# Leaving TensorE's order to the scheduler instead of the program text, in a hybrid attention encoder step

## The chip, the cores and the metric

The kernel runs on one core of a Trainium2 chip, as one launch. The metric is device time in microseconds (us) from the first to the last instruction of the program with what lies around it; a run's time is that of its slowest core, here the only one.

## What is computed

One step of a one-layer streaming encoder in float32, for 1024 prompt frames and 64 sample frames (which also see 512 cached frames), width 1024:

```python
h = x + 0.5 * rmsnorm(swiglu(rmsnorm(x, g_pre_ff1), w_gate1, w_up1, w_down1), g_post_ff1)
u = rmsnorm(h, g_pre_mix) @ w_in                 # 256 + 128 + 32 + 3*512 columns
# group A, 8 heads: latent attention, softmax over chunk-causal scores
s = (q_lat @ latent.T + q_rope @ krope.T) * MLA_SCALE
o_mla = softmax(where(visible, s, -inf)) @ latent @ w_uv
# group B, 8 heads: stick-breaking attention, strictly causal
z = (q @ k.T) * SB_SCALE
tail = reverse_cumsum(log_sigmoid(-z)) - log_sigmoid(-z)
o_sb = where(before, exp(log_sigmoid(z) + tail), 0) @ v
h = h + rmsnorm(concat(rmsnorm(o_mla), rmsnorm(o_sb)) @ w_out, g_post_mix)
h = h + 0.5 * rmsnorm(swiglu(rmsnorm(h, g_pre_ff2), w_gate2, w_up2, w_down2), g_post_ff2)
y = rmsnorm(h, g_final)                          # and the new cache rows
```

The feed-forward width is 2816. Each swiglu is down(silu(gate) * up).

## The kernel before

**Tiling.** The frames are split into two groups: G1 of 576 (512 prompt, 64 sample) in columns of 288, and G2 of 512. Features lie on the 128 partitions, frames along the free dimension. Each float32 product is made of three fp32r matmuls of a high and a low part (`mm3`, `steps`: hi x hi, hi x lo, lo x hi); a weight tile `wr` comes from HBM, ACT casts it to `wh` (L139) and DVE subtracts to get `wl` (L140).

**Two streams of work.** The feed-forward (`ffn`) is a generator that yields after every matmul; its results go to three PSUM banks of their own, tile `f`. The rest is the mixing work: `finish` (residual and norm sums after a feed-forward), `premix`, `project` (u @ w_in and what hangs on it), `attend` (scores in tile `s`, transposes in `t`, weighted values in `v`), `mix_out` (w_out, residual, norm). It uses the other five banks, handed out in turn by `bank_m`. The program's order is: feed-forward 1 of G1; then mixing of G1 with feed-forward 1 of G2 as filler; then mixing of G2 with feed-forward 2 of G1 as filler; then feed-forward 2 of G2. So the stages follow each other along the span: first feed-forward alone, then project, attention and mix_out of G1 with filler, the same of G2 with filler, then feed-forward alone again.

**The reckoned clock.** The text keeps a time of its own, `self.clock`. Every matmul adds its reckoned duration; every mixing step says when its operands will be there and calls `wait`, which writes filler matmuls until the clock has come that far:

```python
            self.clock += max(n / 2400 + 0.013, 0.11)
...
    def wait(self, t):
        while self.clock < t:
            mark = self.clock
            if next(self.filler, BLOCKED) is BLOCKED:
                self.clock = max(t, mark)
...
    def evict(self, n):
        self.busy = max(self.busy, self.clock) + SLACK * (n / 960 + 0.15)
        self.free[self.turn] = self.busy + 0.3
```

`chain` (L639) gives the reckoned time after which a score bank is free again, `took` (L650) the time after which transposes have been read. At the end of a stage the filler can be blocked: `prep2` (L1143), which makes the input of feed-forward 2 of G1, needs the sum `rx` that `mix_out` ends with.

**Who sets the order.** The kernel is written for a layer that records all instructions, finds their dependencies and then gives each engine its order. For DVE, ACT, POOL and SP a scheduler in that layer picks the order: it runs through the recorded program with durations that it assumes, and whenever an engine is free it takes, of the instructions whose operands it holds for ready, the one that was written first. `tc.manual_schedule(engines={PE})` in `build` (L1269) exempts TensorE: its matmuls stand in exactly the order in which the text wrote them. Every engine executes its own order strictly; an instruction whose operand is late holds up all behind it.

Lines that matter below: `mul` L154 and `turn_over` L158 issue all matmuls and transposes; `stick` L593 (L610, L613 and L619 are its DVE steps, the last two the scan); `weighted` L659 (L679 and L680 read the transposes into `ph` and `pl`, which the `v` matmuls take); `rsqrt` L221 (a matmul with `ones` sums the squares over partitions, as in s<-rx,ones); `residual` L272 (the DMA of L275 into tile `e`, the additions of L277).

Of the kernel before, what the change touches and what calls it, by code (L numbers as in the profile page):

```python
# [1261 lines left out]
def build(nc, arrays):  # L1262
    a = {k: nc.dram_tensor("in_" + k, v.shape, mybir.dt.from_np(v.dtype), kind="ExternalInput").ap()
         for k, v in arrays.items()}
    for k, s in OUTS.items():
        a[k] = nc.dram_tensor("out_" + k, list(s), F32, kind="ExternalOutput").ap()
    a["xT"] = [a["xT0"], a["xT1"]]
    with tile.TileContext(nc) as tc:
        with ExitStack() as ctx, tc.manual_schedule(engines={mybir.EngineType.PE}):  # L1269
            body(tc, a, ctx)  # L1270


# [19 lines left out]
```

## Time and profile before

| what | value |
|---|---|
| runs | 2451.69, 2444.57, 2450.37 us; median 2450.37 us |
| profiled execution | 2446.7 us; its span 2444.9 us |
| PE (matmuls) | 2285.4 us busy, 93% of the span, 13869 instructions |
| PEld (weight loads) | 2057.0 us, 84% |
| DVE, ACT, POOL | 1428.3 us (58%), 1291.1 us (53%), 94.7 us (4%) |
| granted TensorE clock, mean | 0.981 |
| DMA | 268.79 MB, mean 110 GB/s |

The span is from the first to the last instruction; the profiled execution's own time has 1.8 us around it. A busy engine counts every stretch in which at least one of its instructions is under way. A wait in the profile is idle time of an engine, put down to the instruction whose end released the next one.

### The profile page before, as it was taken

What the parts mean: (1) busy time and instruction counts of PE and PEld (TensorE: products, weight loads), DVE (VectorE), ACT (ScalarE), POOL (GpSimd) and SP (SyncE); (2) the same over time, 40 slices, a digit from 0 to 9 for tenths busy, and PEclk for the clock granted to TensorE, in tenths of its full rate; (3) what the DMA queues carried; (4) which work ended last, traced back from release to release, by engine and by line L of the source; (5) the groups of instructions that cost most, each with busy time, mean ns of one, the idle gap of its engine ahead of it and who ended that gap; (6) DMA issues with size and microseconds to landing.
All of it is one profiled execution on the core that took longest, in us unless ns stands there. A gap on an engine that the chain in (4) does not pass through costs nothing. (4 is left out here: it accounts for less than half of the span.)

```text
span 2444.9 us, 37638 instructions
## 1 busy us (share of the span) xinstructions
PE 2285.4 (93%) x13869; PEld 2057.0 (84%) x13869; DVE 1428.3 (58%) x2464; ACT 1291.1 (53%) x2498; POOL 94.7 (4%) x270
## 2 busy tenths in 40 slices
PE   8999999989999999997999999989999989999997
PEld 7999999878977777786788998988889788888885
DVE  6444444763167777745674367877776477444445
ACT  6534333552377777644452478777776345433333
POOL 1000000010000000000110000000000010000001
PEclk9999999999999999998999999999999999999998
DMA  6322222624453343233345532323221324333321
GB/s 205 114 88 84 81 80 86 203 95 149 143 160 112 105 120 114 76 135 121 109 143 176 174 91 72 92 76 103 75 70 57 129 88 128 129 98 97 94 92 35
DMA packets 186614, 268.79 MB, mean 110 GB/s; under 512 B 59216, under 2 KB 68048, under 8 KB 186400
## 3 DMA queue, kind: packets, MB, share of 16 engines
q1 hardware_dynamic: 186432, 266.41, 34.5%
q8 instruction: 109, 1.79, 0.3%
q14 instruction: 73, 0.60, 0.1%
HBM read 227.61 MB, written 40.88 MB: 110 GB/s over the span
## 5 line engine op out<-in xcount | busy, mean ns | idle before, releaser
L154 PE MATMUL f<-xh,wh 128*128 128x288 f32 (+1 forms) x2112 | 698.6, 331 | 3.0 <-ACT xh L139 2.8
L154 PE MATMUL f<-xl,wh 128*128 128x288 f32 (+1 forms) x2112 | 698.5, 331 | 1.9 <-POOL xl L140 0.9
L154 PE MATMUL f<-xh,wl 128*128 128x288 f32 (+1 forms) x2112 | 698.8, 331 | 0.0
L139 ACT CAST wh<-wr 128x512 fp32r<-128x512 f32 x638 | 383.8, 618 | 535.3 <-PE f L154 362.5
L140 DVE TENSOR_TENSOR wl<-wr,wh 128x512 fp32r<-128x512 f32 x638 | 435.0, 695 | 265.6 <-ACT wh L139 229.0
L154 PEld LDWEIGHTS f<-xh,wh 128*128 128x128 f32 x2112 | 400.8, 190 | 33.7 <-ACT xh L139 3.3
L154 PEld LDWEIGHTS f<-xl,wh 128*128 128x128 f32 x2112 | 400.5, 190 | 33.0 <-POOL xl L140 2.9
L154 PEld LDWEIGHTS f<-xh,wl 128*128 128x128 f32 x2112 | 401.2, 190 | 28.7 <-issue 1.5
L154 PE MATMUL f<-hh,wh 128*128 128x288 f32 (+2 forms) x1072 | 351.8, 328 | 3.4 <-ACT hh L139 2.0
L154 PE MATMUL f<-hl,wh 128*128 128x288 f32 (+2 forms) x1072 | 349.9, 326 | 1.4 <-DVE hl L140 1.4
L154 PE MATMUL f<-hh,wl 128*128 128x288 f32 (+2 forms) x1072 | 350.5, 327 | 0.0
L154 PEld LDWEIGHTS f<-hh,wh 128*128 128x128 f32 x1072 | 202.3, 189 | 19.4 <-ACT hh L139 2.6
L154 PEld LDWEIGHTS f<-hl,wh 128*128 128x128 f32 x1072 | 202.3, 189 | 15.9 <-DVE hl L140 2.4
L154 PEld LDWEIGHTS f<-hh,wl 128*128 128x128 f32 x1072 | 202.3, 189 | 13.0 <-issue 0.5
L319 DVE TENSOR_TENSOR y<-f,y 128x288 f32<-128x288 f32 (+2 forms) x248 | 127.5, 518 | 119.9 <-PE f L154 119.3
L364 DVE TENSOR_TENSOR act<-f,act 128x288 f32<-128x288 f32 (+1 forms) x132 | 70.0, 530 | 126.3 <-ACT act L363 126.2
L680 DVE TENSOR_TENSOR pl<-t,ph 128x384 fp32r<-128x384 f32 (+1 forms) x160 | 98.4, 630 | 36.9 <-ACT ph L679 35.9
L154 PE MATMUL v<-pl,v 128*128 128x256 f32 x320 | 89.4, 302 | 31.9 <-DVE pl L680 31.4
L365 DVE TENSOR_TENSOR act<-f,act 128x288 f32<-128x288 f32 (+1 forms) x132 | 70.2, 532 | 66.5 <-PE f L154 62.3
L154 PE MATMUL s<-kh,qh 128*128 128x256 f32 (+3 forms) x224 | 81.8, 367 | 27.5 <-DVE a L619 17.4
L679 ACT CAST ph<-t 128x384 fp32r<-128x384 f32 (+1 forms) x160 | 83.6, 541 | 41.3 <-PE t L158 39.1
L139 ACT CAST hh<-act 128x288 fp32r<-128x288 f32 (+1 forms) x132 | 65.2, 494 | 75.6 <-DVE act L365 75.3
(307 smaller groups left out, 3495.8 us busy)
## 6 DMA issues: line engine op xcount, KB each, us to landing
wr<-in_wg SPq DMA_DIRECT2D x176, 256.0 KB, 3.0
wr<-in_wu SPq DMA_DIRECT2D x176, 256.0 KB, 3.1
wr<-in_wd SPq DMA_DIRECT2D x176, 256.0 KB, 2.9
wr<-in_win SPq DMA_DIRECT2D x44, 256.0 KB, 3.2
kl<-ks SPq DMA_DIRECT2D x64, 128.0 KB, 2.8
wr<-in_wout SPq DMA_DIRECT2D x32, 256.0 KB, 2.9
h<-y SPq DMA_DIRECT2D x16, 288.0 KB, 2.2
p<-in_xT SPq DMA_DIRECT2D x16, 256.0 KB, 3.2
```

The lines of the kernel that those rows point to most:

```text
L139: nc.scalar.copy(hi, x)
L140: eng.tensor_tensor(lo, x, f(hi), op=ALU.subtract)
L154: self.nc.tensor.matmul(out, lhsT=lhsT, rhs=rhs, start=start, stop=stop)
L319: nc.vector.tensor_tensor(yy, ps[:, :C], yy, op=ALU.add)
L364: nc.vector.tensor_tensor(s, pg[:, :C], s, op=ALU.mult)
L365: nc.vector.tensor_tensor(s, pu[:, :C], s, op=ALU.mult)
L679: nc.scalar.copy(ph[:, end:], tr[:, end:])
L680: nc.vector.tensor_tensor(pl[:, end:], tr[:, end:], f(ph[:, end:]), op=ALU.subtract)
```

## The change

One line: TensorE is no longer exempt. The scheduler now also gives TensorE its order, by the same rule as the other engines: of the matmuls that it holds for ready, the one that the text wrote first. The text, its reckoned clock, the pools, the banks and the tasks are the same, so the same 13686 matmuls are recorded in the same order; that order is now a priority.

```diff
     with tile.TileContext(nc) as tc:
-        with ExitStack() as ctx, tc.manual_schedule(engines={mybir.EngineType.PE}):
+        with ExitStack() as ctx:
             body(tc, a, ctx)
```

What it moves: on TensorE no matmul stands more than 65 places behind its old place and none over 96 ahead of it, but for 35 filler matmuls that now stand 163 to 384 places earlier, at the start of the two mix_outs. In all, 332 runs of one or more matmuls stand earlier than the text has them. The first feed-forward (places 100 to 3098) and the last (12300 to 13500) keep their order. The orders of DVE and ACT change too (by up to 41 places), since the scheduler makes them together with TensorE's; SP's by up to 27.

Three places follow, with the tile numbers of the two programs (those of the change are lower by 2 for the same tile). The first is TensorE at the end of mix_out of G1, where the norm sum of `rx` is taken; before:

```order
L154 MATMUL f_12111<-xh_100,wh_12103 128x512
L154 MATMUL f_12111<-xl_101,wh_12103 128x512
L154 MATMUL f_12111<-xh_100,wl_12102 128x512
L154 MATMUL s_12159<-rx_4982,ones_69 128x288 x2
L154 MATMUL f_12111<-xh_100,wh_12103 128x512
L154 MATMUL f_12111<-xl_101,wh_12103 128x512
```

and now:

```order
L154 MATMUL f_12285<-hh_11205,wh_12268 128x512
L154 MATMUL f_12285<-hl_11206,wh_12268 128x512
L154 MATMUL s_12157<-rx_4980,ones_67 128x288
L154 MATMUL f_12285<-hh_11205,wl_12267 128x512
L154 MATMUL f_12285<-hh_11372,wh_12274 128x512
L154 MATMUL f_12285<-hl_11373,wh_12274 128x512
L154 MATMUL s_12157<-rx_4980,ones_67 128x288
```

The two sums stood in the middle of the gate product f_12111; 62 feed-forward matmuls that stood behind them (the rest of that product, and down products up to the one in tile f_12285) now stand ahead of the first.

The second is TensorE in the attention of G1, at a score group (`s`) of the last head; before:

```order
L154 MATMUL f_10970<-hh_10099,wh_10848 128x512
L154 MATMUL f_10970<-hl_10100,wh_10848 128x512
L154 MATMUL s_10990<-kh_10647,qh_10653 128x384
L154 MATMUL s_10990<-kl_10646,qh_10653 128x384
L154 MATMUL f_10970<-hh_10099,wl_10847 128x512
```

and now:

```order
L154 MATMUL f_11086<-hh_9165,wh_11031 128x512
L154 MATMUL f_11086<-hl_9166,wh_11031 128x512
L154 MATMUL s_10988<-kh_10645,qh_10651 128x384
L154 MATMUL s_10988<-kl_10644,qh_10651 128x384
L154 MATMUL f_11086<-hh_9165,wl_11030 128x512
```

The group stands 30 places later in the whole order, three down products further on in the filler.

The third is DVE in the attention of G2, where `pl` is made for the weighted values (L613 is the scan); before:

```order
L610 SCALAR_TENSOR_TENSOR a_16828<-z_16829,a_16828 128x640
L140 TENSOR_TENSOR hl_16667<-act_16861,hh_16666 128x288
L613 SCALAR_TENSOR_TENSOR a_16828<-z_16829,a_16828 128x639
L680 TENSOR_TENSOR pl_16909<-t_16907,ph_16908 128x512
L680 TENSOR_TENSOR pl_16918<-t_16916,ph_16917 128x512
```

and now:

```order
L140 TENSOR_TENSOR hl_16665<-act_16859,hh_16664 128x288
L680 TENSOR_TENSOR pl_16907<-t_16905,ph_16906 128x512
L610 SCALAR_TENSOR_TENSOR a_16826<-z_16827,a_16826 128x640
L680 TENSOR_TENSOR pl_16916<-t_16914,ph_16915 128x512
L613 SCALAR_TENSOR_TENSOR a_16826<-z_16827,a_16826 128x639
```

The first `pl` stood behind both steps of the scan; it now stands ahead of both, and the second ahead of the scan itself. The `v` matmuls that take them keep their place on TensorE here.

## Rows read from the trace of the kernel before

**Rows 1.** The profile page, part 1: busy time, share of the span, instructions.
```profile
PE 2285.4 (93%) x13869; PEld 2057.0 (84%) x13869; DVE 1428.3 (58%) x2464; ACT 1291.1 (53%) x2498; POOL 94.7 (4%) x270
```

**Rows 2.** Busy time by stretch: length, then engines' us and counts, granted clock, DMA.
```profile
0.00:470.00 470.00, 460.61 (x3305) 449.62 (x3306) 235.35 (x431) 206.58 (x418) 14.45 (x17) 0.99 0.35 112
470.00:690.00 220.00, 202.40 (x1267) 183.31 (x1267) 87.65 (x137) 87.26 (x167) 10.49 (x11) 0.99 0.44 145
690.00:1025.00 335.00, 308.79 (x1625) 250.06 (x1625) 252.22 (x530) 243.53 (x566) 17.18 (x117) 1.00 0.38 112
1025.00:1110.00 85.00, 79.95 (x510) 73.27 (x509) 36.48 (x60) 35.31 (x67) 0.10 (x1) 0.98 0.35 116
1110.00:1200.00 90.00, 72.42 (x306) 58.18 (x305) 53.70 (x76) 36.29 (x63) 6.52 (x4) 0.91 0.36 114
1200.00:1395.00 195.00, 182.24 (x1059) 161.43 (x1058) 105.39 (x169) 84.97 (x165) 13.01 (x8) 0.98 0.50 160
1395.00:1865.00 470.00, 434.49 (x3107) 416.74 (x3106) 353.81 (x577) 354.53 (x633) 14.01 (x93) 0.98 0.27 83
1865.00:1975.00 110.00, 105.94 (x619) 95.01 (x618) 60.73 (x99) 55.60 (x101) 2.83 (x5) 0.96 0.33 110
1975.00:2100.00 125.00, 111.21 (x621) 98.66 (x620) 88.76 (x142) 58.47 (x102) 9.38 (x7) 0.95 0.38 123
2100.00:2445.00 345.00, 327.36 (x1467) 270.74 (x1465) 154.22 (x248) 128.55 (x223) 6.79 (x8) 0.97 0.27 84
```

**Rows 3.** PE's waits over the span, by releaser: us in total, times, longest us.
```profile
PE v L154 <- DVE pl L680: 31.4, 28, 3.3
PE s L154 <- DVE rx L218: 23.3, 2, 15.5
PE s L154 <- DVE a L619: 17.4, 22, 1.2
...
PE s L154 <- ACT a L635: 9.2, 13, 1.5
...
PE t L154 <- DVE tmp L218: 4.5, 1, 4.5
PE t L154 <- issue: 4.1, 1, 4.1
```

**Rows 4.** Timeline, end of mix_out of G1: start us, us, engine, instruction, [idle before].
```profile
1140.82 1.40 POOL L277 TENSOR_TENSOR y<-y,e 128x576 f32<-128x576 f32 x1 [16.25 <-DMA e<-h]
...
1152.72 1.33 PE L154 MATMUL s<-rx,ones 128*128 128x288 f32 x2 [15.51 <-DVE rx L218]
...
1157.04 0.63 PE L154 MATMUL f<-xh,wh 128*128 128x512 f32 x1
1157.47 0.63 PE L154 MATMUL f<-xl,wh 128*128 128x512 f32 x1
...
1160.70 0.39 PE L154 MATMUL f<-hh,wl 128*128 128x512 f32 x1
1160.92 0.39 PE L154 MATMUL f<-hh,wh 128*128 128x512 f32 x1
...
1205.22 0.67 ACT L139 CAST xh<-tmp 128x576 fp32r<-128x576 f32 x1
```

**Rows 5.** Timeline, attention of G1, a score group and what releases it.
```profile
1008.89 0.69 DVE L619 TENSOR_TENSOR_SCAN a<-s,a 128x255 f32<-128x255 f32 x1
...
1009.72 0.41 PE L154 MATMUL s<-kh,qh 128*128 128x384 f32 x1 [0.84 <-DVE a L619]
```

**Rows 6.** Timeline, attention of G2, the place of the third order above.
```profile
1603.38 0.57 ACT L679 CAST ph<-t 128x512 fp32r<-128x512 f32 x1
...
1603.73 0.82 DVE L610 SCALAR_TENSOR_TENSOR a<-z,a 128x640 f32<-128x640 f32 x1
...
1604.83 1.48 DVE L613 TENSOR_TENSOR_SCAN a<-z,a 128x639 f32<-128x639 f32 x1
1606.23 1.26 DVE L680 TENSOR_TENSOR pl<-t,ph 128x512 fp32r<-128x512 f32 x2
...
1606.95 0.39 PE L154 MATMUL v<-pl,v 128*128 128x256 f32 x1 [3.06 <-DVE pl L680]
```

## The prediction

> **What bounds the kernel now.** I read the page's busy times first: PE works 93% of the span, DVE 58%, ACT 53% [rows 1]. So the time is TensorE's work plus TensorE's idle time. The work is the same 13686 matmuls before and after; what the change can alter is the idle time and the clock that the work runs at.
>
> Second, the stretches, because a mean over stages hides where the idle time lies. Length less PE busy gives, in the order of [rows 2]: 9.4, 17.6 (project of G1), 26.2 (attention of G1), 5.1 (mix_out of G1), 17.6 (its end), 12.8 (finish and project of G2), 35.5 (attention of G2), 4.1, 13.8 (mix_out of G2 and its end), 17.6 us (the last feed-forward and the tail): 159.6 us in all. The most that an order could win is about 160 us less what no order can fill, the start and the end.
>
> Third, what the waits are for [rows 3]. In the attention of G2 the `v` matmuls wait for `pl` from DVE, 28 times for 31.4 us. In that of G1 the score matmuls wait for a bank that the scan or the exponential still reads (17.4 and 9.2 us, 35 times). Two norm sums wait for `rx`, 23.3 us. All are alike: the text's clock held an operand for ready, wrote the matmul, and TensorE stood still although filler lay behind it.
>
> **What the change does to each.** It adds and removes no instruction, no DMA and no bank; it only moves. A matmul that the scheduler holds for late is overtaken by filler. So I set each wait against the work put ahead of it. Work is counted at the full clock: a 512-column matmul starts 0.22 us after the one before it [rows 4], the pair at 1160.7; 0.226 over longer runs, a 288-column one after about 0.14 us, 460.6 us by 3305 in the first stretch [rows 2].
>
> *End of mix_out of G1, 17.6 us.* 62 matmuls of 512 columns now stand ahead of the sum: 62 x 0.226 = 14.0 us against a wait of 15.5. But the norm sum before it, t<-acc, stands 15 places later too, so the new cover since then is 47 x 0.226 = 10.6 us, and the residual chain that ends in `rx` waits for its own DMA, e<-h [rows 4], so it does not shorten. Bounds 10.6 and 15.5; I take 11, nearest to the first. What is late next: the input of feed-forward 2, whose last cast ran at 1205 us [rows 4] while its matmuls had begun. That cast waits for the buffer of the other group's input, thus for filler that is itself moved forward, so it moves along.
>
> *Attention of G2, 35.5 us.* Two things help. Before most `v` groups stand 2 to 9 matmuls of 0.14 us now, 0.3 to 1.2 us against waits of some 0.9. Where none do, DVE's order has changed: in [rows 6] `ph` was there at 1603.95, `pl` came only after both steps of the scan (0.82 and 1.48 us), and TensorE stood 3.06 us. Now `pl` is made ahead of them. The scan is delayed in turn; what it feeds is the score chain, which has room here: nearly all score groups of this stage start without a wait (2 of the waits on L635 lie here, 2.6 us). Bounds: 18 us if only the moved matmuls count, each wait against the work ahead of it, 33 if nearly all goes. I take 28, since of the waits without a moved matmul, some 13 us, nearly all are at places where DVE's order has changed in this way.
>
> *Attention of G1, 26.2 us.* Here the gain is smaller than it looks. A score group starts 0.14 us after the scan that frees its bank ends at 1009.58, then 1009.72 [rows 5], and so do most others: the chain score, scan, score sets the pace, and filler put ahead can be counted once, not at each wait. By the last head a score group stands 30 places later: 30 x 0.226 = 6.8 us of filler done early. I take 7; bounds 0 and 17, the sum of each wait against all that stands ahead of it.
>
> *Project of G1, 17.6 us.* Ahead of a waiting product stand 3 to 9 matmuls of the next product or of filler, 0.4 to 1.2 us, against waits mostly of 0.5 to 1; three larger ones keep more than half. I take 8, bounds 0 and 15.
>
> *Finish and project of G2, 12.8 us.* The two norm sums (waits of 4.1 us [rows 3] and 3.0) get 30 and 25 matmuls of 0.14 us ahead, 4.2 and 3.5 us. I take 10, bounds 0 and 12.8.
>
> *Mix_outs and the end of G2's.* G1's mix_out, 5.1 us: 2 (0 to 5). G2's, 4.1 us: 3 (0 to 4). The end of G2's, 13.8 us: 61 matmuls of 288 columns, 8.5 us, ahead of the sum that waited 23.3 - 15.5 = 7.8 us, and 10 ahead of one that waited 4.5: together 11 (0 to 13). Start and tail hardly move: 1 (0 to 2).
>
> Sum: 11 + 28 + 7 + 8 + 10 + 2 + 3 + 11 + 1 = 81 us; ends 29 and 117.
>
> *The clock.* [...] As the waits go, I take 12 back, about half, since some waits stay. Ends 0 and 22.
>
> *New waits.* 332 runs of matmuls, counted in the two orders, stand earlier than before. Where the scheduler holds an operand for ready and it is not, TensorE now waits there. A wait of the usual size is 17.4 / 22 = 0.8 us [rows 3]; one run in 25 gives 13 x 0.8 = 10 us. That is the loss I take, an estimate, ends 0 and 50: the weights and hidden tiles that filler needs are made well ahead in this trace.
>
> Net 81 + 12 - 10 = 83 us. From the profiled execution, 2446.7 us: **2364 us**. That execution lies 3.7 us below the median of the runs, 2450.4, within their spread of 7.
>
> [...] In the attention of G1, TensorE goes through all its banks in turn and stands still 26.2 us in short pieces, yet the granted clock is 1.00 [rows 2]. [...]
>
> **The rivals.**
> 1. *The mixing chain sets the pace in more places.* For it: [rows 5], and the residual chain with its DMA [rows 4]. Then filler put ahead is only counted once per stage and the waits come back further on. The lower ends, 29 us, with 5 of clock: 2447 - 34 = 2413, between 2400 and 2435. Against it: in the attention of G2 the score groups hardly wait. Chance 0.14.
> 2. *Slower: the scheduler is early more often than the text was.* The text's times carry margins; the scheduler's rule has none, and on one in-order queue a filler matmul whose bank or weight is late holds up the score chain behind it. The price is 0.8 us each [rows 3]; it decides from 93 / 0.8 = 116 of the 332 runs, one in three. At 133 it is 106 us, 2447 - 93 + 106 = 2460. Against it: DVE and ACT are at most 75% busy in any stretch [rows 2], and where the trace has a wait the order mostly puts about as much ahead as the wait is long, so the scheduler's times look near the real ones. Chance 0.11.
> 3. *The clock swings.* If the granted clock fell to 0.90 in both attentions, 0.10 x 335 + 0.08 x 470 = 71 us go, and the 12 of clock: 2364 + 83 = 2447, no change. Against it: 1.00 in [rows 2]. Chance 0.04.
> 4. *Nothing comes of it*: the order moves as shown, but DVE, which gets the filler's work sooner, is late by as much. 2447; chance 0.03. That the change does nothing at all is excluded by the orders shown.
>
> **How the numbers follow.** The forecast has 0.68 and a range of its own from 2330 to 2400 (sum 117 at best; 0 new waits and part of the clock, or 50 of new waits). With rival 1 that is 0.82, less the tails: range 2330 to 2435. A difference of 0.3%, 7 us, is about what a measurement of this kernel can tell from none. Faster: 0.68 + 0.14 = 0.82. Same: 0.04 + 0.03 = 0.07. Slower: 0.11.
>
> **What would show it.** Right: the two waits s<-rx fall from 23.3 to under 7 us; those for `pl` from 31.4 to under 8; those of the scores in the attention of G1 stay at 15 to 22; the clock in 1110 to 1200 is above 0.96; total idle time of PE near 85 us. Rival 1: the waits for `pl` stay above 15. Rival 2: new waits of `f` matmuls for a cast or a bank, tens of us in sum. Rival 3: a granted clock under 0.95 in the attentions. The prediction is wrong if PE's busy time itself changes by more than the clock explains.

## The result, and the profile after

The changed kernel takes 2364.19 us (median of 4 runs, 2362.49 to 2366.24); beside it the kernel before took 2449.78 us (2444.57 to 2451.69). The ratio is 0.9654, with a 95% interval of 0.9637 to 0.9671: 86 us less. The forecast was 2364.0 us. As will be seen, the sum came out right while two of its largest terms were wrong in opposite directions.

The profiled execution took 2364.98 us, with a span of 2363.2 us. The page's busy times after, against [rows 1]:

```profile
PE 2276.1 (96%) x13869; PEld 2045.5 (87%) x13869; DVE 1427.0 (60%) x2468; ACT 1282.0 (54%) x2494; POOL 94.2 (4%) x270
```

The instructions of PE are as many as before, and its busy time fell by 9.3 us, with a mean granted clock of 0.989 for 0.981; the rest of the 82 us is idle time that is gone. The stretches of [rows 2] start earlier now, since time was saved ahead of them. So the same view is cut here at the places where the same steps of the mixing work begin; only the cut at 1002 lies some 4 us of mixing work too early (columns as in [rows 2]):

```profile
0.00:472.00 472.00, 461.57 (x3294) 450.21 (x3295) 232.91 (x427) 206.42 (x418) 14.49 (x17) 0.99 0.35 110
472.00:685.00 213.00, 205.62 (x1279) 186.48 (x1277) 92.34 (x144) 86.02 (x163) 9.95 (x12) 0.98 0.47 154
685.00:1002.00 317.00, 309.70 (x1627) 249.98 (x1628) 251.31 (x530) 239.72 (x565) 17.15 (x117) 1.00 0.41 118
1002.00:1086.00 84.00, 81.84 (x533) 74.81 (x532) 38.85 (x65) 40.06 (x75) 0.10 (x1) 1.00 0.38 124
1086.00:1158.00 72.00, 67.52 (x287) 54.34 (x286) 51.24 (x75) 33.38 (x57) 6.50 (x4) 0.98 0.43 135
1158.00:1346.00 188.00, 178.98 (x1052) 157.69 (x1052) 105.43 (x167) 83.38 (x162) 12.15 (x8) 1.00 0.51 164
1346.00:1795.00 449.00, 431.06 (x3107) 410.77 (x3106) 348.76 (x572) 351.82 (x632) 14.22 (x93) 1.00 0.29 87
1795.00:1898.00 103.00, 100.80 (x611) 91.03 (x610) 61.63 (x102) 54.09 (x100) 2.56 (x4) 1.00 0.35 113
1898.00:2019.00 121.00, 111.57 (x634) 100.07 (x633) 91.20 (x147) 58.92 (x104) 10.26 (x7) 0.96 0.42 131
2019.00:2363.00 344.00, 327.48 (x1462) 270.08 (x1460) 153.28 (x246) 128.21 (x222) 6.78 (x8) 0.98 0.27 85
```

Length less PE busy gives the idle time of each stage, row by row, beside what the prediction had for it:

| stage | idle before | idle after | gain | forecast |
|---|---|---|---|---|
| feed-forward 1 of G1 | 9.4 | 10.4 | -1.0 | with the tail, 1 |
| project of G1 | 17.6 | 7.4 | 10.2 | 8 |
| attention of G1 | 26.2 | 7.3 | 18.9 | 7 |
| mix_out of G1 | 5.1 | 2.2 | 2.9 | 2 |
| its end | 17.6 | 4.5 | 13.1 | 11 |
| finish and project of G2 | 12.8 | 9.0 | 3.7 | 10 |
| attention of G2 | 35.5 | 17.9 | 17.6 | 28 |
| mix_out of G2 | 4.1 | 2.2 | 1.9 | 3 |
| its end | 13.8 | 9.4 | 4.4 | 11 |
| last feed-forward, tail | 17.6 | 16.5 | 1.1 | see first row |
| sum | 159.6 | 86.9 | 72.7 | 81, less 10 of new waits |

72.7 us of idle time and 9.3 us of busy time are the 82 us. PE's waits after, against [rows 3] (us in total, times, longest us):

```profile
PE v L154 <- DVE pl L680: 13.3, 25, 1.5
PE f L154 <- ACT t L238: 11.6, 4, 4.3
PE f L154 <- DVE y L319: 8.0, 3, 6.6
...
PE t L158 <- ACT a L624: 4.8, 5, 1.6
PE s L154 <- DVE a L619: 4.5, 11, 0.7
...
PE s L154 <- DVE rx L218: 3.6, 1, 3.6
...
PE s L154 <- ACT a L635: 0.6, 1, 0.6
```

The waits of the scores for their bank (L619 and L635) went from 26.6 us to 5.1, those for `rx` from 23.3 to 3.6, those for `pl` only from 31.4 to 13.3. Two lines stand high in the list that were small or absent before: a feed-forward matmul that waits for an addition on DVE (8.0 us, nearly all of it one wait of 6.6; it was 0.5), and transposes that wait for ACT (4.8; none before).

How a wait went can be seen at one score group of the attention of G1, in the timeline of the changed kernel:

```profile
982.80 1.22 DVE L619 TENSOR_TENSOR_SCAN a<-s,a 128x511 f32<-128x511 f32 x1
...
983.44 0.39 PE L154 MATMUL f<-hh,wh 128*128 128x512 f32 x1
983.66 0.39 PE L154 MATMUL f<-hl,wh 128*128 128x512 f32 x1
984.16 0.36 PE L154 MATMUL s<-kh,qh 128*128 128x256 f32 x1
```

The scan that frees the bank ends at 984.02 and the score group starts 0.14 us later, as in [rows 5]. But no wait is marked on the group's row: feed-forward matmuls ran nearly until then. The group starts 0.50 us after the matmul before it, where those start 0.22 us apart, so that it lost at most 0.3 us, against a wait of 0.84 in [rows 5].

The one new wait, in the feed-forward that fills the end of mix_out of G2. DVE's rows there, then PE's one:

```profile
1915.67 0.45 DVE L319 TENSOR_TENSOR y<-f,y 128x288 f32<-128x288 f32 x1
1916.04 1.49 DVE L263 SCALAR_TENSOR_TENSOR e<-h,c_gains,rx 128x512 f32<-128x512 f32 x1
1917.45 0.68 DVE L140 TENSOR_TENSOR xl<-e,xh 128x512 fp32r<-128x512 f32 x1
1918.06 3.08 DVE L263 SCALAR_TENSOR_TENSOR e<-h,c_gains,rx 128x512 f32<-128x512 f32 x3
...
1924.16 1.18 DVE L319 TENSOR_TENSOR y<-f,y 128x288 f32<-128x288 f32 x3
```

```profile
1924.66 0.61 PE L154 MATMUL f<-hh,wh 128*128 128x288 f32 x1 [6.65 <-DVE y L319]
```

The additions of L319 empty the PSUM banks of the feed-forward. Between 1916.1 and 1924.2 none ran: DVE made the input of the last feed-forward (L263 and L140) first. The matmul at 1924.66 waited 6.65 us for a bank.

### The profile page after: what moved, and what is told of

The parts are those of the page before. It is cut to its first block, busy times and chain, and to the rows that moved or that the text cites. A ratio compares the mean times of both kernels' runs of the same rounds, so it can differ in the third digit from the quotient of the medians.

```text
span 2363.2 us, 37608 instructions
## 1 busy us (share of the span) xinstructions
PE 2276.1 (96%) x13869; PEld 2045.5 (87%) x13869; DVE 1427.0 (60%) x2468; ACT 1282.0 (54%) x2494; POOL 94.2 (4%) x270
## 4 chain that ended last, share of the span: by engine, by line
PE 71%; DVE 11%; ACT 9%; DMA 5%; issue 3%; POOL 1%; SPq 0%; DVEq 0%; ACTq 0%; POOLq 0%
PE f L154 48%; PE s L154 9%; PE v L154 6%; PE t L154 6%; DVE a L613 2%; PE t L158 2%; ACT wh L139 1%; DVE wl L140 1%; ACT a L607 1%; ACT a L609 1%; ACT a L608 1%; DVE a L610 1%; DVE e L263 1%; DVE pl L680 1%; DMA e<-h 1%
## 5 line engine op out<-in xcount | busy, mean ns | idle before, releaser
L140 DVE TENSOR_TENSOR wl<-wr,wh 128x512 fp32r<-128x512 f32 x638 | 435.9, 698 | 250.6 <-ACT wh L139 217.8
L154 PEld LDWEIGHTS f<-xh,wl 128*128 128x128 f32 x2112 | 398.2, 189 | 28.4 <-issue 1.7
L154 PEld LDWEIGHTS f<-hl,wh 128*128 128x128 f32 x1072 | 202.7, 189 | 14.6 <-issue 1.0
L154 PEld LDWEIGHTS f<-hh,wl 128*128 128x128 f32 x1072 | 202.8, 189 | 13.8 <-issue 1.0
L319 DVE TENSOR_TENSOR y<-f,y 128x288 f32<-128x288 f32 (+2 forms) x248 | 126.9, 517 | 121.7 <-PE f L154 121.3
L680 DVE TENSOR_TENSOR pl<-t,ph 128x384 fp32r<-128x384 f32 (+1 forms) x160 | 98.6, 631 | 28.6 <-ACT ph L679 27.4
L154 PE MATMUL v<-pl,v 128*128 128x256 f32 x320 | 89.8, 303 | 14.2 <-DVE pl L680 13.3
L158 PE MATMUL t<-c_ident,a 128*128 128x128 f32 x616 | 91.3, 273 | 4.9 <-ACT a L624 4.8
```

The source lines that it names most:

```text
L140: eng.tensor_tensor(lo, x, f(hi), op=ALU.subtract)
L154: self.nc.tensor.matmul(out, lhsT=lhsT, rhs=rhs, start=start, stop=stop)
L158: self.nc.tensor.transpose(out, x, ident)
L319: nc.vector.tensor_tensor(yy, ps[:, :C], yy, op=ALU.add)
L680: nc.vector.tensor_tensor(pl[:, end:], tr[:, end:], f(ph[:, end:]), op=ALU.subtract)
```

## The experiments

The same kernel takes a slightly different time in each set of runs, and the sets ran on more than one chip: the changed kernel was run again beside later experiments and took 2359.22 us (2358.38 to 2359.86), with 2446.62 us for the kernel before there, a ratio of 0.9644 [0.9631, 0.9657]. Two kernels that did not run in the same set are therefore compared by their ratios to the kernel before, and by the idle time of PE in a stage. "The scheduler's order" is that of the changed kernel, "the text's order" that of the kernel before.

### The text's order in one attention alone

The changed kernel, with the text's order on TensorE while the attention of one group is written:

```diff
-    with tc.tile_pool(name="a0", bufs=2) as ap:
+    with tc.tile_pool(name="a0", bufs=2) as ap, tc.manual_schedule(engines={mybir.EngineType.PE}):
         L.attend(ap, 0)
```

> TensorE keeps the text's order in the attention of G1 alone; the scheduler orders the rest. Theory A, each stage's gain is its own: the stage from 690 us on, 22 us shorter after the change, goes back, about 2364 + 20 = 2384 us, with the waits of the scores for the scan near 17 us again. Theory B, the prediction's reckoning that only some 7 us come from this stage: 2371 us. Theory C, the filler that the stage does early is what counts and is made up for later: 2364 us.

Measured: 2378.98 us, ratio 0.9736 [0.9719, 0.9752]. Against the two ratios of the changed kernel, 0.9654 and 0.9644, that is 0.8 to 0.9% or 20 to 22 us more. The waits of the scores for their bank are back, and the attention of G1 has its old length:

```profile
PE s L154 <- DVE a L619: 17.0, 21, 1.2
...
PE s L154 <- ACT a L635: 5.4, 9, 1.0
```

```profile
683.00:1016.00 333.00, 308.27 (x1625) 250.08 (x1624) 252.53 (x529) 243.28 (x564) 17.27 (x118) 1.00 0.37 111
```

1625 matmuls in 333 us, where [rows 2] has 1625 in 335. The changed kernel, cut at the same steps as this run:

```profile
687.00:1006.00 319.00, 311.45 (x1641) 251.37 (x1640) 253.75 (x533) 241.40 (x567) 17.15 (x117) 1.00 0.41 118
```

It does as much, and 16 filler matmuls more, in 14 us less. So the order in this attention is worth about 20 us, not my 7.

The same for the attention of G2 (`a1`):

> TensorE keeps the text's order in the attention of G2 alone. Theory A, the stage's idle time goes back from 18 to about 35 us and the clock with it (17.6 + 5): about 2386 us. Prediction's size of this term, 28 + 6: 2398 us. Rival, what helped here was DVE's order, which does not need TensorE's to be free: about 2374 us and waits for pl under 20 us.

Measured: 2381.11 us, ratio 0.9739 [0.9725, 0.9754], 21 to 23 us more by the ratios. The waits for `pl` are back at their old size:

```profile
PE v L154 <- DVE pl L680: 31.5, 27, 3.3
```

This stage's idle time is 35.5 us, 17.6 more than in the changed kernel: less than I had forecast for it, but nearly as much as the attention of G1 gives. (The scheduler makes the orders of the other engines together with TensorE's; no run changes TensorE's order with DVE's held fixed.)

### The text's order everywhere but in the attentions

The reverse: TensorE has the text's order from the start to the first attention, between the two, and after the second.

```diff
+    text = tc.manual_schedule(engines={mybir.EngineType.PE})
+    text.__enter__()
...
+        text.__exit__(None, None, None)
     with tc.tile_pool(name="a0", bufs=2) as ap:
         L.attend(ap, 0)
```

> The text's order on TensorE everywhere but in the two attentions, which are left to the scheduler. Theory A (the gains of the stages add up): the runs with the text's order in one attention alone cost 15 and 17 us, so this one gains about 32 of the 81 us over the kernel before, about 2413 us; the rx waits stay near 23 us. Rival (the attentions' gain needs the order around them): under 16 us of gain, above 2429 us.

Measured: 2409.73 us, ratio 0.9852 [0.9833, 0.9871], which is 36 us of the gain. The attentions have 6.4 and 19.0 us of idle time, as in the changed kernel, and the `rx` waits are 21.8 us, as before. (The 32 us of the expectation came from times of different sets of runs; the ratios of the two runs above sum to 41 to 45.) The stages add up, nearly: 36 to 45 of the 86 us come from the attentions, and the rest from the other stages.

### DVE's order alone

The change also moved DVE's order, and the prediction had laid half of the gain in the attention of G2 on that. `tc.high_priority()` lets the scheduler take what is written in it ahead of other instructions that are ready. First in the kernel before, whose TensorE keeps the text's order:

```diff
-            nc.scalar.copy(ph[:, end:], tr[:, end:])
-            nc.vector.tensor_tensor(pl[:, end:], tr[:, end:], f(ph[:, end:]), op=ALU.subtract)
+            with self.tc.high_priority():
+                nc.scalar.copy(ph[:, end:], tr[:, end:])
+                nc.vector.tensor_tensor(pl[:, end:], tr[:, end:], f(ph[:, end:]), op=ALU.subtract)
```

> TensorE in the text's order throughout; only the two instructions that read the transposes into ph and pl are given a higher priority on ACT and DVE, so that pl stands ahead of the scan wherever both are ready. If DVE's order is worth what the prediction held of it, the 13 us of waits for pl that no moved matmul covered go, and some clock: 2450 - 15 = 2435 us, waits for pl about 18 us. If the moved matmuls did it all: no change, 2450 us, and the scan that is late costs score waits instead.

Measured: 2440.47 us, ratio 0.9982 [0.9968, 0.9995]. Its waits (the edit moves L680 to L681):

```profile
PE s L154 <- DVE a L619: 18.7, 23, 1.7
PE s L154 <- ACT a L635: 16.5, 14, 4.9
...
PE t L158 <- ACT a L624: 8.9, 9, 2.5
PE v L154 <- DVE pl L681: 7.6, 13, 1.7
```

The waits for `pl` fall from 31.4 to 7.6 us, 23.8 less, and the kernel is 4.7 us faster, 0.2%, a third of the 15 us expected. Other waits grew: the scores' for a bank that L635, the exponential of the softmax heads, still reads, by 7.3 us, and transposes wait 8.9 us for L624, the exponential behind the scan. That DVE is late with the scan because of `pl` is not what the trace shows: ahead of those waits of the transposes the scan's first step starts within 0.03 us of the ACT step before it, and no `pl` stands between that step and the scan. From the copy of the scores (L604) to the end of the scan the 32 groups of this stage take 272 us in all, 266 before. TensorE comes sooner to the next thing that it needs of this chain; the chain is no faster, so TensorE waits there. (The priority covers ACT's copy too; the run does not tell its effect from that of DVE's subtraction.)

Then the same edit in the changed kernel:

> The changed kernel, with priority on VectorE and ScalarE for the copy and the subtraction that make the low half pl, so that they run as soon as they are ready. Theory A (what is left of the pl waits, 13.3 us in 25 waits, is VectorE taking the subtraction late): the pl waits fall under 5 us and the time to about 2357 us. Rival: the vector work that the subtraction overtakes is the score chain's own, and its waits grow by as much: 2362 to 2370 us.

Measured: 2363.15 us, ratio 0.9661 [0.9647, 0.9676], no difference from the changed kernel. `pl` waits fall from 13.3 to 8.0 us, those for L624 rise from 4.8 to 12.1: the rival's outcome, waits that move. The 13.3 us that stayed are not to be had by moving `pl` ahead.

### The size of the reckoned clock

Is what matters that the scheduler gives the order, or how much filler stands ahead of each step? First in the kernel before, with a text that reckons with later operands, so that it writes more filler ahead of each step:

```diff
-EASE = 0.8
+EASE = 2.0
...
-            return self.took(2.4), j, ph, pl, order
+            return self.took(3.4), j, ph, pl, order
...
-        self.wait(t + 2.0)
+        self.wait(t + 20.0)
```

> TensorE in the text's order, but the text's clock holds three things for later: transposes read after 3.4 us instead of 2.4, score banks free 1.2 us later, and the residual's last sum 18 us later at the end of mix_out. If the waits came from times in the text that were too early by about their own length, most of the 31 us for pl, the 26 us for score banks and the 23 us for rx are filled by filler and the time falls to about 2390 us without the scheduler. Rival: a later clock delays also those steps that were on time, so the chain is stretched and the waits come back elsewhere: 2430 to 2450 us.

Measured: 2444.42 us, ratio 0.9999 [0.9990, 1.0009]. That is the rival's range. The waits in the attentions nearly went (`pl` 7.4 us, L619 5.3), as the larger margins intend. But the idle time came back elsewhere, most of it as one kind of wait: `rx` has 54.9 us, 31.6 more than before, the longest 33.9. Its stretches of the attention of G1, and of the end of mix_out of G1:

```profile
694.00:1077.00 383.00, 375.13 (x1937) 315.49 (x1936) 284.22 (x577) 270.14 (x608) 16.93 (x117) 0.98 0.39 117
...
1158.00:1226.00 68.00, 28.59 (x115) 23.10 (x115) 40.65 (x57) 24.46 (x43) 9.84 (x6) 0.65 0.27 89
```

1937 matmuls ran in the attention, 312 more than in [rows 2]; they are missing at the end, where PE works 28.6 of 68 us and the clock is 0.65. Filler is finite in a stage, since the next feed-forward's input hangs on `rx`. Margins between these and the old ones were not tried, so it is not shown that no text does better.

Then the changed kernel with a later and with an earlier clock (shown: the later one; the earlier has SLACK 0.9 and EASE 0.0):

```diff
-SLACK = 1.15
+SLACK = 1.4
...
-EASE = 0.8
+EASE = 1.6
```

> The changed kernel with a later reckoned clock (SLACK 1.4 for 1.15, EASE 1.6 for 0.8), the other side of the run with an earlier one (2372 us). Theory A (the scheduler's own readiness starts what is due late, so only filler taken too early does harm): within 5 us of the changed kernel, 2359 to 2369 us. Rival (the clock holds filler back too long, as it did with the text's order): the score chain or the mixing chain starts late, 2372 us or more, with waits at the end of the first mix_out.

Measured: 2381.36 us, ratio 0.9737 [0.9723, 0.9751]; the changed kernel took 2359.22 beside it: 22 us slower, the rival's figure, though the expectation has the filler the wrong way round. A later clock writes more filler ahead of each step, not less. The rows show it, attention and end of mix_out of G1, then attention and mix_out of G2:

```profile
688.00:1040.00 352.00, 347.15 (x1824) 289.79 (x1823) 271.49 (x557) 258.29 (x591) 17.21 (x117) 1.00 0.39 116
...
1122.00:1184.00 62.00, 33.65 (x142) 26.06 (x142) 40.95 (x58) 25.08 (x47) 10.80 (x6) 0.72 0.31 103
...
1365.00:1855.00 490.00, 475.38 (x3461) 457.41 (x3460) 370.38 (x618) 369.76 (x667) 14.19 (x93) 1.00 0.28 86
1855.00:1972.00 117.00, 94.64 (x537) 83.14 (x536) 73.94 (x126) 55.12 (x96) 7.76 (x5) 0.91 0.35 116
```

The attentions idle less than in the changed kernel (4.9 and 14.6 us against 7.3 and 17.9), the end of mix_out of G1 28.4 against about 5, and the mix_out of G2 22.4 against about 2. It is the picture of the run before it, at a smaller size, under the other order.

> The changed kernel with a more optimistic reckoned clock (SLACK 0.9 for 1.15, EASE 0.0 for 0.8), so that filler matmuls are due earlier against the score chain. Theory A (the scheduler's readiness decides, and the clock's size matters little): within 6 us of the changed kernel, 2358 to 2370 us. Rival: the numbers are what spreads the filler, and with filler due sooner it runs out before the attention ends: score waits of several us each return, 2375 us or more.

Measured: 2372.33 us, ratio 0.9698 [0.9680, 0.9715], some 11 to 13 us more than the changed kernel by the ratios and between the two expectations. Here too the expectation has the sense reversed: an earlier clock writes less filler ahead, and filler is left over. The end of mix_out of G2 is filled now, and the attention of G2 idles more, 23.7 us:

```profile
1338.00:1749.00 411.00, 387.31 (x2714) 363.77 (x2713) 324.44 (x527) 335.39 (x594) 14.33 (x92) 0.99 0.28 85
...
1862.00:2027.00 165.00, 162.67 (x1042) 151.93 (x1043) 109.70 (x182) 79.70 (x148) 9.24 (x6) 1.00 0.36 115
```

Over the span its idle time is the changed kernel's (2370.4 - 2283.1 = 87.3 us against 2363.2 - 2276.1 = 87.1); the loss in this profile lies in PE's busy time, 7.0 us more, at granted clocks of 0.97 to 0.99 in stretches where the changed kernel has 1.00. Neither theory had that. The granted clock fell in two places there, at a wait of 3.5 us for `act` (0.53 from 1619 to 1630 us) and at one of 5.0 for L319 (0.66 from 1839 to 1849). PE was busy for 44.3 us at a granted clock of 0.50, against 37.1 in the changed kernel; by these times I put half of the 7.0 us down to the clock, an estimate, and the other half is open.

So the numbers in the text still matter under the scheduler: they are its priorities, and a move to either side cost time.

### The one new wait

The changed kernel, with priority on the additions that empty PSUM in the feed-forward:

```diff
-                nc.vector.tensor_tensor(yy, ps[:, :C], yy, op=ALU.add)
+                with self.tc.high_priority():
+                    nc.vector.tensor_tensor(yy, ps[:, :C], yy, op=ALU.add)
```

> The changed kernel, with priority on the feed-forward's additions that empty PSUM (L319). Theory A (the new wait of 6.65 us of a feed-forward's first matmul for that addition is VectorE's order): the waits of f for y fall from 8.0 us to under 2 and the time to about 2357 us. Rival: the additions push back the vector chain that the next residual or scan waits for, which moves the wait: 2362 us or more.

Measured: 2356.86 us, ratio 0.9633 [0.9618, 0.9648]. Since two sets of runs of one kernel differ by nearly as much, both kernels were run again side by side:

> The changed kernel itself once more, beside the others on the same chip: 2362 to 2366 us, ratio 0.965 to 0.967.

> The changed kernel with priority on the feed-forward's additions (L319) once more, to be compared with the changed kernel on the same chip. Theory A (the wait of 6.65 us and the stretch of matmuls at the lower clock behind it, some 2.5 us, are gone): 6 to 9 us under the changed kernel. Rival (the two earlier results differ by the chip): within 2 us of it.

Measured: 2359.22 us (2358.38 to 2359.86) for the changed kernel, 2356.07 us (2354.03 to 2356.91; ratio 0.9630 [0.9617, 0.9643]) with the additions first. The ranges do not overlap: 3.2 us faster, between the two expectations. DVE's rows there, of the second run (L319 is L320 now):

```profile
1916.42 0.45 DVE L320 TENSOR_TENSOR y<-f,y 128x288 f32<-128x288 f32 x1
1916.78 0.74 DVE L263 SCALAR_TENSOR_TENSOR e<-h,c_gains,rx 128x512 f32<-128x512 f32 x1
1917.44 0.68 DVE L140 TENSOR_TENSOR xl<-e,xh 128x512 fp32r<-128x512 f32 x1
1918.05 0.45 DVE L320 TENSOR_TENSOR y<-f,y 128x288 f32<-128x288 f32 x1
```

The additions now stand between the steps of the chain, and `f<-y` waits fall from 8.0 to 2.7 us. That is the whole theory, wait and slow stretch, and it should have given some 7 us; part is given back in the attentions, whose idle times are 10.0 and 21.0 us against 6.9 and 18.7 in the changed kernel beside it: the waits for `pl` are 17.0 us against 13.1, those for the scan (L620 here) 6.4 against 4.6. That additions stand ahead of `pl` there is a guess; in the waits for `pl`, additions ran in four of them in either kernel.

Last, both priorities together:

> The changed kernel with priority both on the additions that empty PSUM in the feed-forward (L319) and on the copy and subtraction that make pl. Theory A (VectorE's order takes what it is asked to, and waits only move): the part with pl brings nothing again, 2355 to 2358 us. Rival (with the additions first, pl waits had risen to 17.3 us, and the second priority takes these back): 2346 to 2352 us.

Measured: 2357.76 us (2353.19 to 2358.95), ratio 0.9630 [0.9616, 0.9644], no better than the additions alone. `pl` waits fall to 4.2 us, those for L624 are 13.3: the waits only move, as in the earlier runs with this priority. The kernel with the additions first is the fastest of the study, by a little.

## Why the prediction was right, and where it was not

**The frame held.** TensorE's work stayed, its idle time was what the change could alter, and filler stood behind most waits. Idle time fell by 72.7 us, where the terms less new waits gave 71; PE's busy time fell by 9.3 us, where I took 12 for the clock. No run shows that 12, nor the end of 22 beside it. What the runs showed: a mean granted clock of 0.989 for 0.981 beside the 9.3 us, and, in the kernel before, 0.50 from 1141 to 1157 us, in the long wait for `rx` and behind it, where the changed kernel has 0.98 over that stage. The signs named beforehand: `rx` under 7 (3.6, seen), the granted clock near the first `rx` above 0.96 (0.98, seen), idle time near 85 us (86.9, seen), `pl` under 8 (13.3, not seen), score waits of the attention of G1 staying at 15 to 22 (4.9 us by L619 and L635 there, not seen).

**Attention of G1, 7 forecast, 18.9 measured.** The step that failed is "filler put ahead can be counted once, not at each wait". Its premise, that the chain score, scan, score sets the pace, holds for a part of the stage only. The score groups come in four stretches of stick-breaking heads, whose banks the scan frees, and between them three of softmax heads. One stretch of each, cut at the first and last start of L607, the first ACT step of a stick-breaking group; before:

```profile
808.10:852.60 44.50, 39.78 (x202) 31.63 (x200) 34.12 (x69) 35.94 (x81) 2.30 (x18) 1.00 0.34 101
852.60:894.40 41.80, 40.33 (x227) 33.55 (x225) 31.27 (x70) 28.94 (x72) 2.21 (x13) 1.00 0.41 117
```

and after:

```profile
798.50:843.20 44.70, 43.94 (x223) 35.01 (x222) 34.42 (x69) 35.51 (x83) 2.30 (x18) 1.00 0.40 119
843.20:879.40 36.20, 35.59 (x201) 29.14 (x200) 29.25 (x63) 27.05 (x68) 2.18 (x13) 1.00 0.40 111
```

The four stick-breaking stretches together take 175.2 us before and 176.5 after, though 452 filler matmuls ran in them before and 507 after, and their idle time fell from 18.9 to 5.1 us. There the chain does set the pace. The three softmax stretches, in which PE was busy 96% of the time, take 125.5 us before and 112.5 after, with 280 and 249 filler matmuls. So filler done in the waits of the one kind is taken off the other, where TensorE's own work sets the pace, and each wait counts by itself, as in the upper bound of 17. (Of the 26.6 us of score waits that the prediction laid in this stage, 2.6 lie in the attention of G2.)

**Attention of G2, 28 forecast, 17.6 measured.** The step that failed is that "nearly all" of some 13 us of waits without moved matmuls would go, because DVE makes `pl` ahead of the scan. It does at the place of [rows 6], and the 3.06 us there are 1.13 now:

```profile
1547.79 0.39 PE L154 MATMUL v<-pl,v 128*128 128x256 f32 x1 [1.13 <-DVE pl L680]
```

But the runs with priority for `pl` show that an earlier `pl` alone gains little: in the kernel before, 23.8 us of `pl` waits went and the time fell by 4.7 us. The lower end of this term, 18, which counted moved matmuls only, agrees with the measured 17.6. "What it feeds is the score chain, which has room here" was not so for the transposes behind L624.

**Finish and project of G2, 10 forecast, 3.7 measured.** The two norm sums did gain: the wait of 4.1 us is 1.6 now, and that of 3.0 is not in the list. Other matmuls wait there in their place (feed-forward ones 2.7 us for `act` and 0.9 for `xl`, a later norm sum 1.3).

**The end of mix_out of G2, 11 forecast, 4.4 measured.** The `rx` wait of 7.8 us went as forecast, that of 4.5 shrank to 2.3; the 6.65 us for L319 are new. This is the mechanism of rival 2, a filler matmul whose bank is late, in one place and not in a third of 332. New waits in the whole: 7.5 us more for L319 and 4.8 for L624; with the smaller lines that grew (`act` 2.5, `xh` 1.6, `xl` 1.3, the norm sums' 1.3, L622 1.1 and others) some 20 us, where I had allowed 10. In the table they are already taken off the gains of their stages. **Project of G1, the mix_outs and the first end** came within 2.2 us of their terms.

**Rivals.** Rival 1 falls: its time was 2400 to 2435 us, and in the stage that spoke for it each wait did count. Rival 4, no change, is excluded by the time. Rival 3: the granted clock did not fall to 0.90 in the attentions. Banks are handed out in turn there all along, and the trace after has 1.00 over the 317 and the 449 us of these stages, with no wait over 1.6 us. The evidence is not all on one side. The attention of G2 before, with waits of up to 3.3 us, had 0.98 [rows 2]. And with the additions first the granted clock fell once in the attention of G1, to 0.62 over 4.5 us, where no wait from 700 us on was over 0.7 us:

```profile
719.00:723.50 4.50, 4.50 (x18) 3.85 (x18) 3.37 (x9) 3.21 (x8) 0.00 (x0) 0.62 0.47 119
```

That the total came out so close is partly luck: the two attentions were off by +11.9 and -10.4 us, finish and the last end by -6.3 and -6.6, the clock by -2.7, and the 10 us for new waits covered most of the last two.

## What to carry to other kernels

Leaving an order to a scheduler pays where idle time is scattered in small waits and independent work is at hand behind each: here it won 3.5% without a new instruction, while the one set of larger margins tried in the hand-written order only moved the idle time to the place where the filler was used up. A chain whose steps follow each other promptly can set the pace in one part of a stage and not in the next. So look at the parts one by one: filler done in the chain's waits is worth its time when it is taken off a part where TensorE's own work sets the pace. After such a change, look for the one long new wait, and at the order of the engine that it names; giving one operand priority can just move the wait to the next thing that TensorE needs, as here with `pl`.

## What the runs showed of the hardware

A long wait cost more than its length here. Four short stretches of the changed kernel, ahead of the 6.65 us wait, in it, behind it and later (columns as in [rows 2]):

```profile
1911.70:1917.70 6.00, 6.00 (x46) 5.83 (x45) 5.49 (x9) 4.52 (x10) 1.29 (x1) 1.00 0.15 45
1917.70:1924.60 6.90, 0.32 (x3) 0.09 (x1) 5.74 (x9) 2.95 (x5) 3.55 (x3) 0.70 0.00 0
1924.60:1930.60 6.00, 5.94 (x25) 5.94 (x26) 3.25 (x7) 0.00 (x0) 1.04 (x1) 0.50 0.39 131
1930.60:1936.60 6.00, 6.00 (x46) 6.00 (x46) 3.01 (x7) 2.18 (x4) 0.00 (x0) 0.99 0.01 3
```

In the 6 us behind the wait the granted clock is 0.50, and 25 matmuls run where 46 ran before and after: 21 matmuls at 0.13 us, or 2.7 us on top of the wait. With the additions first the same stretch has a granted clock of 1.00 and 47 matmuls:

```profile
1924.60:1930.60 6.00, 6.00 (x47) 5.94 (x46) 5.14 (x9) 1.65 (x3) 1.29 (x1) 1.00 0.35 103
```

The small waits in the attention of G2, 17.9 us in 449 and none over 1.6, went with a granted clock of 1.00; before, with 35.5 us of waits of up to 3.3, it was 0.98.
